# Feed-forward opening of a two-layer hybrid network: the casts of the first four weight units leave the pinned order of ACT

## The chip, the cores and the metric

The kernel runs on one core of a Trainium2 chip. The metric is the device time of one execution in microseconds (us); of several executions the median counts. The core has five engines with an instruction queue each: PE (TensorE, the matrix products; a separate row PEld shows its weight loads), DVE (VectorE), ACT (ScalarE), POOL (GpSimd) and SP (SyncE, which here only issues DMA transfers). Each engine executes its own queue in order, and engines wait for one another by semaphores.

## The reference, cut to what matters

Two layers work on 512 latent tokens and 256 context tokens of width 1024. Layer 0 mixes the tokens with an mLSTM and gated linear attention, layer 1 with an RWKV-7 recurrence. After each mixer stands a residual with two norms, and then a gated feed-forward part with a 3x3 depthwise convolution on the gate; the change touches that part's opening.

```python
def conv_ffn(h, w_up, conv_w, conv_b, w_down, grid):
    gate, up = jnp.split(h @ w_up, 2, axis=-1)
    gate = dwconv_grid(gate, conv_w, conv_b, grid)
    return (jax.nn.gelu(gate, approximate=True) * up) @ w_down

# reference(), per layer
xl = xl + mod_l[2] * rmsnorm(yl, norm_g[layer, 1])
hl = modulate(rmsnorm(xl, norm_g[layer, 2]), mod_l[3], mod_l[4])
xl = xl + mod_l[5] * rmsnorm(conv_ffn(hl, ffn_w_up[layer], ffn_conv_w[layer], ffn_conv_b[layer],
                                      ffn_w_down[layer], lat_grid), norm_g[layer, 3])
```

In layer 0 the context tokens go through the same steps; in layer 1, the last, only the latent tokens do. The width of gate and up is 2816 each.

## The kernel before, in words

**Layout.** Activations lie with the width on the 128 partitions: 8 tiles of 128 rows, the tokens along the free axis. The tokens are cut into three segments of 256 columns: CTX (context), H0 and H1 (the halves of the latent tokens). Layer 0 works on CTX, H0, H1 in this order, layer 1 on H0, H1.

**Products in three parts.** Every fp32 value is split into a high part (a cast to the matrix engine's rounded type) and a low part (value minus high part). A product is the sum of three matmuls: high by high, high weights by low activations, low weights by high activations. Activations are `mh`/`ml` in layer 0 and `zh`/`zl` in layer 1.

**A weight unit** (`unit`) is 1024 x 128 weights: SP issues the load of `wraw` (L390), ACT casts it to `whi` in two halves of 128x512 (L396), and DVE or POOL subtracts to `wlo` in two halves (L397). There are 15 buffers for such units.

**Two kinds of order.** The program is written out once, and a scheduler places the instructions of each engine by its own estimates, within the data dependences. `Ordered` is a wrapper around the engines: an ACT call made through it is handed to `keep_in_program_order`, and such ACT instructions keep the order in which they are written, among themselves; in the profile their line is that of the wrapper, L220. All other instructions are placed freely.

**The end of a mixer** (`passes`). The mixer's output projection (matmuls into `po`) goes segment by segment, and within a segment over eight output tiles m. At m = 0 of a segment the residual of the segment before is posted, at m = 7 its second norm; the last segment's residual and norm come after all products. A residual or norm begins with `rstd`: ones-matmuls add squares over the partitions (L555), DVE adds a constant (L558), POOL takes the power (L559), PE spreads the result (L561); for a norm ACT copies it (L565). The residual is then L620 and L621 (DVE, every third L621 on POOL), a store of the new stream to `xd` (L623, on SP), squares on ACT (L626) and their pair sums (L630, POOL and DVE). The norm makes the high and low parts: L590 on DVE, L594, L595, L599 on ACT, L597 on POOL, L601 on DVE. The squares for the first norm are summed on the way (L574, L577 on ACT, L578 on POOL).

**The opening burst of the feed-forward part** (`ffn`, L1094, with `projn`). Two blocks of 128 gate columns and the two matching up blocks are computed at once, so that one pass over a segment's activations serves four weight units (`UP_FIRST` = 2): units 0 and 2 subtract on DVE, 1 and 3 on POOL (`PROJN_LO`). For each segment there are 4 units x 8 tiles x 3 = 96 matmuls of 256 columns (L434, L435, L436), into PSUM tiles `pjC` (context) and `pjL` (latent). That is 288 matmuls in layer 0 and 192 in layer 1. The gate is then copied into a padded tile (`pc` or `pl`, in `act`), filtered, and put through the gelu. After the burst come the steps: blocks of up-projection (`up`) and of down-projection (`down`), with each step's weights fetched one step ahead (`fetch`).

**What is pinned before.** The wrapper is made at the top of `ffn`. So the eight casts of the opening's four units are pinned ACT instructions, as are all ACT instructions of the feed-forward part after them; those of the mixer's end before them are not.

Of the kernel before, what the change touches and what calls it, by code (L numbers as in the profile page):

```python
# [305 lines left out]
class Net:  # L306
# [787 lines left out]
    def ffn(self, layer, xh, xl, segs, y, ss, xd, post):  # L1094


        plain, I = self.nc, self.I
        nc = self.nc = Ordered(plain, self.tc)
        fw = lambda f, i: self.v("fcw", (layer * 9 + i) * NF + f, 1)
        both = len(segs) == 3  # L1100
        wide = SEGS if both else (LAT,)
# [4 lines left out]
        def act(f, acc, key, pg, pu):  # L1106
            o, w = (LAT if key == "L" else CTX)[:2]
            pl, pc = pads[f % 2]
            a = acc[:, o:o + w]
            if key == "L":  # L1110
                nc.scalar.copy(pl[:, 1:9, 1:65], pg.rearrange("p (r c) -> p r c", c=64))
                b = a.rearrange("p (r c) -> p r c", c=64)
                taps = [(i, pl[:, i // 3:i // 3 + 8, i % 3:i % 3 + 64]) for i in range(9)]
            else:
                nc.scalar.copy(pc[:, 1:257], pg[:, :w])
                b = a
                taps = [(3 + i, pc[:, i:i + 256]) for i in range(3)]
            for n, (i, src) in enumerate(taps):
                if n == 0:
                    nc.scalar.activation(b, src, AF.Identity, scale=fw(f, i), bias=self.v("fcb", layer * NF + f, 1))  # L1120
                    yield
                else:
                    nc.vector.scalar_tensor_tensor(b, src, fw(f, i), b, op0=ALU.mult, op1=ALU.add)  # L1123
            nc.scalar.activation(a, a, AF.Gelu_apprx_tanh)
            yield
            nc.vector.tensor_tensor(a, a, pu[:, :w], op=ALU.mult)

        def whole(f, acc, keys, pgs, pus):

            acts = [act(f, acc, key, pgs[key], pus[key]) for key in keys]  # L1130
            for a in acts:
                next(a)
            yield
            for a in acts:
                next(a)
            for a in acts:
                drain(a)
            h, l = self.sl("gh", dt=F32R), self.sl("gl", dt=F32R)
            gate[f] = h, l
            h, l, a = h[:, o0:T], l[:, o0:T], acc[:, o0:T]  # L1140
            nc.scalar.copy(h, a)
            yield
            (nc.gpsimd if f % 2 else nc.vector).tensor_tensor(l, a, h.bitcast(F32), op=ALU.subtract)
            done.add(f)
        live, done = [], set()

        def advance(new=None):
            k = list(live)
            if new is not None:
                next(new)  # L1150
                live.append(new)
            for g in k:
                if next(g, drain) is drain:
                    live.remove(g)
        def fetch(f0, nf, m):

            if nf:
                return self.unit(I["down"][layer, m, :, f0 * P:(f0 + nf) * P], n=nf * P)
            return [self.unit(I["up"][layer, f0, i], PROJN_LO[i]) for i in range(2)]
# [22 lines left out]
        n = UP_FIRST  # L1182
        accs = [self.sl("fa") for _ in range(n)]
        for key, psts in self.projn([I["up"][layer, i // 2, i % 2] for i in range(2 * n)], xh, xl, segs, UP_TAGS[layer]):
            if key == "C":
                acts = [act(f, accs[f], key, psts[2 * f], psts[2 * f + 1]) for f in range(n)]
                for _ in range(3):
                    for a in acts:
                        next(a, None)
                continue  # L1190
            ws = fetch(*steps[0])
            for f in range(n):
                advance(whole(f, accs[f], "L", {"L": psts[2 * f]}, {"L": psts[2 * f + 1]}))
# [952 lines left out]
```

## Time and profile before

| | |
|---|---|
| executions (three) | 2747.04, 2759.9, 2769.5 us; median 2759.9 |
| the profiled execution | 2768.18 us, of which 2766.2 us are the span |
| mean granted clock of PE | 0.939 of full speed |
| DVE busy | 1605.3 us (58%) |
| ACT busy | 1057.3 us (38%) |
| POOL busy | 970.0 us (35%) |
| read from memory, written | 213.61 MB, 37.89 MB; 91 GB/s over the span |

Below, a timeline row gives the start, the duration, the engine, the line, the operation with its output and inputs, the number of instructions drawn together, and in square brackets the engine's idle time before it with what ended that. "PE <-ACT whi L220" reads: PE was idle until ACT's cast at L220 was done. SPq rows are the issue of DMA transfers by SP. A row of windows gives a stretch's start and end, its length, the busy time of PE, PEld, DVE, ACT and POOL with the number of instructions, the granted clock of PE, the share of the DMA engines and the GB/s.

### The profile page before, as it was taken

What the parts mean: (1) busy time and instruction counts of PE and PEld (TensorE: products, weight loads), DVE (VectorE), ACT (ScalarE), POOL (GpSimd) and SP (SyncE); (2) the same over time, 40 slices, a digit from 0 to 9 for tenths busy, and PEclk for the clock granted to TensorE, in tenths of its full rate; (3) what the DMA queues carried; (4) which work ended last, traced back from release to release, by engine and by line L of the source; (5) the groups of instructions that cost most, each with busy time, mean ns of one, the idle gap of its engine ahead of it and who ended that gap; (6) DMA issues with size and microseconds to landing.
All of it is one profiled execution on the core that took longest, in us unless ns stands there. A gap on an engine that the chain in (4) does not pass through costs nothing. (4 is left out here: it accounts for less than half of the span.)

```text
span 2766.2 us, 47123 instructions
## 1 busy us (share of the span) xinstructions
PE 2529.3 (91%) x18916; PEld 2040.7 (74%) x18916; DVE 1605.3 (58%) x2915; ACT 1057.3 (38%) x2205; POOL 970.0 (35%) x1031
## 2 busy tenths in 40 slices
PE   5889999878899999997989879999999998799998
PEld 2677777767888888886756647576768777678886
DVE  4567757734554464747465374665565554676774
ACT  4543443444333232334343233433443443443332
POOL 2443355444222322246212251322222212344425
PEclk8999999998899999997999989999999998899999
DMA  6221234341212212132234453333322222333323
GB/s 226 73 83 60 70 106 146 99 159 52 78 54 59 87 37 78 54 126 73 90 109 151 153 135 80 89 86 98 86 45 65 47 69 85 107 92 94 90 84 107
DMA packets 195667, 254.57 MB, mean 92 GB/s; under 512 B 112120, under 2 KB 127864, under 8 KB 195448
## 3 DMA queue, kind: packets, MB, share of 16 engines
q1 hardware_dynamic: 195448, 251.56, 30.2%
q8 instruction: 149, 2.44, 0.4%
q14 instruction: 70, 0.57, 0.1%
HBM read 213.61 MB, written 37.89 MB: 91 GB/s over the span
## 5 line engine op out<-in xcount | busy, mean ns | idle before, releaser
L397 POOL TENSOR_TENSOR wlo<-wraw,whi 128x512 fp32r<-128x512 f32 (+1 forms) x393 | 543.2, 1404 | 890.7 <-ACT whi L220 454.8
L1123 DVE SCALAR_TENSOR_TENSOR fa<-pl,vec,fa 128x512 f32<-128x512 f32 x352 | 331.3, 948 | 181.4 <-ACT fa L220 175.0
L233 POOL TENSOR_SCALAR_AFFINE_SELECT T<-T 64x256 f32<-64x256 f32 x192 | 98.3, 514 | 270.9 <-ACT T L233 227.4
L220 ACT CAST whi<-wraw 128x512 fp32r<-128x512 f32 (+1 forms) x288 | 149.3, 581 | 68.0 <-DMA wraw<-in_up 26.2
L396 ACT CAST whi<-wraw 128x512 fp32r<-128x512 f32 x241 | 139.0, 619 | 74.0 <-DMA wraw<-in_wmod 22.2
L397 DVE TENSOR_TENSOR wlo<-wraw,whi 128x512 fp32r<-128x512 f32 x136 | 115.5, 887 | 77.8 <-ACT whi L220 34.0
L220 ACT COPY pl<-pjL 128x512 f32<-128x512 f32 x44 | 25.8, 586 | 339.4 <-PE pjL L412 304.0
L408 PE MATMUL pjL<-zh,whi 128*128 128x512 f32 x320 | 126.2, 394 | 2.2 <-ACT whi L220 2.2
L409 PE MATMUL pjL<-ml,whi 128*128 128x512 f32 x320 | 126.6, 396 | 0.0
L409 PE MATMUL pjL<-zl,whi 128*128 128x512 f32 x320 | 126.3, 395 | 0.0
L412 PE MATMUL pjL<-zh,wlo 128*128 128x512 f32 x320 | 126.1, 394 | 0.1
L408 PE MATMUL pjL<-mh,whi 128*128 128x512 f32 x320 | 126.1, 394 | 0.0
L412 PE MATMUL pjL<-mh,wlo 128*128 128x512 f32 x320 | 126.0, 394 | 0.0
L233 DVE TENSOR_SCALAR SU<-cst,el 64x64 f32<-64x64 f32 x176 | 51.1, 291 | 116.2 <-PE cst L233 113.1
L412 PE MATMUL pdL<-gh,wlo 128*128 128x512 f32 x288 | 113.8, 395 | 1.0 <-POOL wlo L397 1.0
L408 PE MATMUL pdL<-gh,whi 128*128 128x512 f32 x288 | 113.3, 394 | 0.2 <-ACT whi L220 0.2
L409 PE MATMUL pdL<-gl,whi 128*128 128x512 f32 x288 | 113.2, 393 | 0.0
L1175 DVE TENSOR_TENSOR y<-y,pdL 128x512 f32<-128x512 f32 x48 | 33.0, 687 | 108.3 <-PE pdL L412 108.2
L233 PE MATMUL pmy<-T,q0t 64*64 64x192 f32 x768 | 94.1, 349 | 0.8 <-DVE SU L233 0.8
L233 ACT ACTIVATE SU<-cst,el 64x64 f32<-64x64 f32 x176 | 53.6, 307 | 104.1 <-PE cst L233 103.6
L233 PE MATMUL ps<-bk,av 64*64 64x192 f32 x768 | 89.5, 355 | 3.5 <-DVE bk L233 1.9
L408 PE MATMUL pjC<-mh,whi 128*128 128x256 f32 x320 | 89.8, 281 | 0.0
(502 smaller groups left out, 7328.1 us busy)
## 6 DMA issues: line engine op xcount, KB each, us to landing
wraw<-in_up SPq DMA_DIRECT2D x88, 512.0 KB, 3.6
wraw<-in_wmod SPq DMA_DIRECT2D x64, 512.0 KB, 4.0
wfill<-in_wmod SPq DMA_DIRECT2D x32, 512.0 KB, 5.1
wraw<-in_rkv SPq DMA_DIRECT2D x24, 512.0 KB, 3.8
wraw<-in_win_fm SPq DMA_DIRECT2D x21, 512.0 KB, 4.4
wraw<-in_down SPq DMA_DIRECT2D x32, 320.0 KB, 2.9
xd<-y SPq DMA_DIRECT2D x64, 128.0 KB, 1.8
wraw<-in_down SPq DMA_DIRECT2D x32, 256.0 KB, 2.6
```

The costliest lines, as they stand in the source:

```text
L220: return lambda *a, **k: self.tc.keep_in_program_order(f(*a, **k))
L233: return f(*a, **k)
L396: nc.scalar.copy(hi[:, c], raw[:, c])
L397: (nc.gpsimd if lo == "pool" else nc.vector).tensor_tensor(w[:, c], raw[:, c], hi[:, c].bitcast(F32), op=ALU.subtract)
L408: nc.tensor.matmul(pst[tag][:m, :w], w1, xh[kc][:, o:o + w], start=st, stop=False)
L409: nc.tensor.matmul(pst[tag][:m, :w], w1, xl[kc][:, o:o + w], start=False, stop=False)
L412: nc.tensor.matmul(pst[tag][:m, :w], w0, xh[kc][:, o:o + w], start=False, stop=sp)
L1123: nc.vector.scalar_tensor_tensor(b, src, fw(f, i), b, op0=ALU.mult, op1=ALU.add)
L1175: nc.vector.tensor_tensor(yj, yj, pst[tag][:, :w], op=ALU.add)
```

## The change

The wrapper is no longer made at the top of `ffn` but inside the loop over the segments of the opening burst, after the first piece of that burst has been written out. `projn` calls `unit` before it yields its first piece, and by then `self.nc` is still the plain one; so the casts of the opening's four units, eight per layer and 16 in all, are not pinned any more (their line becomes L396). In layer 0 the pinned order now begins with the first copy into a pad tile, in layer 1 with the casts of step 0, which are fetched ahead of the first copy.

```diff
     def ffn(self, layer, xh, xl, segs, y, ss, xd, post):
...
-        plain, I = self.nc, self.I
-        nc = self.nc = Ordered(plain, self.tc)
+        I = self.I
+        plain = nc = self.nc
...
         for key, psts in self.projn([I["up"][layer, i // 2, i % 2] for i in range(2 * n)], xh, xl, segs, UP_TAGS[layer]):
+
+            nc = self.nc = Ordered(plain, self.tc)
             if key == "C":
```

No instruction is added or removed. What moves are the casts, and with them the loads, subtractions and matmuls that depend on them, at the opening of both feed-forward parts.

On ACT, in layer 0, around the last norm before the burst; `whi<-wraw` are the casts, `nt`, `mh` the norm of H1, `pc` the first pad copy. Before:

```order
L594 ACTIVATE nt<-nt,modT 128x256
L595 CAST mh<-nt 128x256
L220 CAST whi<-wraw 128x512 x8
L220 COPY pc<-pjC 128x256
L220 ACTIVATE fa<-pc,vec 128x256
```

After, among the work of the output projection's last segment (`y<-po` is its copy out of PSUM, `sq` and `xc` are squares); these are the casts of units 1, 2 and 3, those of unit 0 stand some rows earlier:

```order
L626 ACTIVATE xc<-y 128x256 x2
L396 CAST whi<-wraw 128x512 x2
L626 ACTIVATE xc<-y 128x256 x2
L458 COPY y<-po 128x256
L626 ACTIVATE xc<-y 128x256
L577 ACTIVATE sq<-y 128x256
L458 COPY y<-po 128x256
L577 ACTIVATE sq<-y 128x256
L396 CAST whi<-wraw 128x512 x2
L458 COPY y<-po 128x256
L577 ACTIVATE sq<-y 128x256
L396 CAST whi<-wraw 128x512 x2
```

The eight casts stood in one block behind the last norm; now they stand two by two among the copies and squares of an earlier stretch.

On SP, in layer 0: `xd_94<-y` are the 24 stores of the new stream, `in_up` the loads of the feed-forward weights, of which the first four are the opening's. Before:

```order
L610 DMA xc<-in_xT 128x768 x8
L390 DMA wraw<-in_wout 128x1024 x5
L1086 DMA wraw<-in_wout 128x1024
L390 DMA wraw<-in_up 128x1024
L623 DMA xd_94<-y 128x256 x24
L390 DMA wraw<-in_up 128x1024 x11
```

After:

```order
L390 DMA wraw<-in_up 128x1024
L623 DMA xd_94<-y 128x256 x9
L390 DMA wraw<-in_up 128x1024
L623 DMA xd_94<-y 128x256 x6
L390 DMA wraw<-in_up 128x1024
L623 DMA xd_94<-y 128x256
L390 DMA wraw<-in_up 128x1024 x2
L623 DMA xd_94<-y 128x256 x8
L390 DMA wraw<-in_up 128x1024 x7
```

Three of the opening's loads stood behind all 24 stores; now they stand behind 9, 15 and 16 of them.

On POOL, in layer 0, over the same stretch: `wlo` are the subtractions of units 1 and 3. Before:

```order
L630 TENSOR_TENSOR xc<-xc 128x256
L621 TENSOR_TENSOR y<-y,xc 128x256
L578 TENSOR_TENSOR ss<-ss,sq 128x256 x4
L559 TENSOR_TENSOR rsc<-rsc,powc 128x2 x2
L597 TENSOR_TENSOR ml<-nt,mh 128x256 x4
```

After:

```order
L630 TENSOR_TENSOR xc<-xc 128x256
L397 TENSOR_TENSOR wlo<-wraw,whi 128x512 x2
L621 TENSOR_TENSOR y<-y,xc 128x256
L578 TENSOR_TENSOR ss<-ss,sq 128x256 x3
L397 TENSOR_TENSOR wlo<-wraw,whi 128x512 x2
L578 TENSOR_TENSOR ss<-ss,sq 128x256
L559 TENSOR_TENSOR rsc<-rsc,powc 128x2 x2
```

Unit 1's two halves are now ahead of the last addition of H0's residual, and unit 3's two ahead of the last sum of squares of H1. Units 0 and 2 move on DVE into the same stretch.

On PE, in layer 0, from the end of the output projection; `rsb` are the sums and spreads of `rstd`. Before:

```order
L555 MATMUL rsb<-onek,xc 128x1 x8
L555 MATMUL rsb<-onek,ss 128x1 x2
L561 MATMUL rsb<-ident,rsc 128x128 x2
L555 MATMUL rsb<-onek,ss 128x1 x2
L561 MATMUL rsb<-ident,rsc 128x128 x2
L555 MATMUL rsb<-onek,xc 128x1 x8
L561 MATMUL rsb<-ident,rsc 128x128 x2
L434 MATMUL pjC<-mh,whi 128x256
L435 MATMUL pjC<-ml,whi 128x256
```

After:

```order
L555 MATMUL rsb<-onek,xc 128x1 x8
L555 MATMUL rsb<-onek,ss 128x1 x2
L434 MATMUL pjC<-mh,whi 128x256
L435 MATMUL pjC<-ml,whi 128x256
L436 MATMUL pjC<-mh,wlo 128x256
L434 MATMUL pjC<-mh,whi 128x256
L561 MATMUL rsb<-ident,rsc 128x128 x2
L555 MATMUL rsb<-onek,ss 128x1 x2
L435 MATMUL pjC<-ml,whi 128x256
```

The burst began behind all sums and spreads; now its context products of units 0 and 1 stand between them. Further on in the order after, 15 matmuls of H0 follow, and then the four sums of H1's second norm, with 11, 17 and 6 context matmuls of units 2 and 3 between them, 4 more ahead of their spread, and 10 behind it; the remaining 177 latent matmuls come last.

On PE, in layer 1, at the second norm of H1, its names with their numbers (`pjL_21657` to `pjL_21660` are the four units' tiles, `zh_20581` is the first tile of activations). Before:

```order
L555 MATMUL rsb_21555<-onek_80,xc_21207 128x1 x2
L555 MATMUL rsb_21555<-onek_80,xc_21209 128x1 x2
L555 MATMUL rsb_21555<-onek_80,xc_21211 128x1 x2
L555 MATMUL rsb_21555<-onek_80,xc_21213 128x1 x2
L561 MATMUL rsb_21555<-ident_74,rsc_21564 128x128 x2
L434 MATMUL pjL_21657<-zh_20581,whi_21627 128x256
```

After:

```order
L434 MATMUL pjL_21659<-zh_21137,whi_21643 128x256
L435 MATMUL pjL_21659<-zl_21138,whi_21643 128x256
L436 MATMUL pjL_21659<-zh_21137,wlo_21644 128x256
L555 MATMUL rsb_21555<-onek_80,xc_21207 128x1 x2
L434 MATMUL pjL_21658<-zh_20581,whi_21635 128x256
L435 MATMUL pjL_21658<-zl_20582,whi_21635 128x256
```

The sums stood ahead of the whole burst; now the 48 matmuls of H0 with units 0 and 2 are ahead of them, the 48 with units 1 and 3 between and behind them (7, 18, 6 between the four sums, 4 ahead of the spread, 13 behind it), and the 96 of H1 come last. On POOL and ACT the subtractions and casts of layer 1 move up likewise, to ahead of and among the residual and norm of H0, and on SP four more loads of `in_up` stand ahead of the first stores.

## The prediction

> **What bounds the kernel now.** I began with the page's busy times and then cut the span into windows, since the average says little about a stretch.
>
> ```profile
> PE 2529.3 (91%) x18916; PEld 2040.7 (74%) x18916; DVE 1605.3 (58%) x2915; ACT 1057.3 (38%) x2205; POOL 970.0 (35%) x1031
> ...
> 660.00:671.00 11.00, 11.00 (x96) 11.00 (x94) 2.90 (x5) 4.50 (x12) 6.01 (x8) 1.00 0.18 61
> 676.00:685.00 9.00, 1.22 (x4) 0.93 (x4) 9.00 (x21) 6.36 (x16) 5.22 (x7) 0.50 0.05 18
> 685.00:690.00 5.00, 3.38 (x15) 3.30 (x16) 3.75 (x6) 1.44 (x4) 2.39 (x4) 0.50 0.70 193
> 700.00:707.00 7.00, 6.56 (x30) 6.27 (x31) 6.34 (x4) 3.73 (x8) 6.89 (x7) 0.52 0.23 75
> 705.00:1225.00 520.00, 519.63 (x3056) 458.41 (x3055) 278.18 (x362) 162.57 (x307) 148.10 (x109) 1.00 0.23 71
> 2366.00:2372.00 6.00, 0.00 (x0) 0.00 (x0) 5.19 (x11) 5.26 (x13) 3.82 (x6) 0.50 0.38 156
> 2376.00:2397.00 21.00, 21.00 (x180) 21.00 (x179) 4.51 (x3) 3.06 (x6) 6.90 (x5) 1.00 0.11 37
> 2410.00:2700.00 290.00, 288.76 (x1241) 232.81 (x1242) 211.79 (x238) 112.27 (x206) 118.91 (x89) 1.00 0.31 92
> ```
>
> PE bounds it: 91% of the span, and practically all of 705 to 1225 and of 2410 to 2700, the two feed-forward parts. Just before each of them PE is nearly idle at half clock: 1.22 of 9.00 us, 3.38 of 5.00, 0 of 6. Since PE is full behind these gaps, whatever the opening burst gains reaches the end of the kernel one to one; the gaps are what to look at.
>
> The timelines of PE, ACT, POOL and SP there:
>
> ```profile
> 671.24 1.84 PE L555 MATMUL rsb<-onek,xc 128*128 128x1 f32 x16
> 674.67 0.51 PE L555 MATMUL rsb<-onek,ss 128*128 128x1 f32 x4
> 676.48 1.22 PE L561 MATMUL rsb<-ident,rsc 128*128 128x128 f32 x4 [1.31 <-POOL rsc L559]
> 685.18 1.87 PE L555 MATMUL rsb<-onek,xc 128*128 128x1 f32 x8 [7.47 <-POOL xc L630]
> 688.48 1.87 PE L555 MATMUL rsb<-onek,xc 128*128 128x1 f32 x8 [1.44 <-DVE xc L630]
> 691.46 1.22 PE L561 MATMUL rsb<-ident,rsc 128*128 128x128 f32 x4 [1.11 <-POOL rsc L559]
> 700.14 0.58 PE L434 MATMUL pjC<-mh,whi 128*128 128x256 f32 x1 [7.46 <-ACT whi L220]
> ...
> 699.47 2.70 ACT L220 CAST whi<-wraw 128x512 fp32r<-128x512 f32 x5
> 736.76 0.59 ACT L220 COPY pl<-pjL 128x512 f32<-128x512 f32 x1 [18.28 <-PE pjL L436]
> ...
> 2357.39 1.87 PE L555 MATMUL rsb<-onek,xc 128*128 128x1 f32 x8 [9.40 <-POOL xc L630]
> 2363.68 1.22 PE L561 MATMUL rsb<-ident,rsc 128*128 128x128 f32 x4 [1.11 <-POOL rsc L559]
> 2372.34 0.58 PE L434 MATMUL pjL<-zh,whi 128*128 128x256 f32 x1 [7.44 <-ACT whi L220]
> ...
> 2396.03 0.59 ACT L220 COPY pl<-pjL 128x512 f32<-128x512 f32 x1 [17.14 <-PE pjL L436]
> ...
> 658.81 0.92 POOL L597 TENSOR_TENSOR ml<-nt,mh 128x256 fp32r<-128x256 f32 x1
> 662.15 0.92 POOL L621 TENSOR_TENSOR y<-y,xc 128x256 f32<-128x256 f32 x1
> 680.91 1.97 POOL L597 TENSOR_TENSOR ml<-nt,mh 128x256 fp32r<-128x256 f32 x2 [1.60 <-ACT mh L595]
> ...
> 624.66 63.83 SPq L623 DMA_DIRECT2D xd<-y  x24
> 688.59 19.37 SPq L390 DMA_DIRECT2D wraw<-in_up  x6
> ...
> wraw<-in_up SPq DMA_DIRECT2D x88, 512.0 KB, 3.6
> ```
>
> In both layers the burst's first matmul (700.14, 2372.34) waits for ACT's pinned cast, which starts at 699.47, right behind the last norm. The last low part of the context was finished at 659.73 (658.81 + 0.92), H0's at 682.88: PE had data but no weights. And the loads of units 1 to 3 are issued only at 688.59, behind the 24 stores. The end of the burst is the first `pl` copy: 736.76 and 2396.03.
>
> **The casts themselves** (16) cost nothing new: 2.70 us for five, so about 0.54 us each, as before. What hides them is ACT's free time: in 660 to 671 it is busy for 4.50 of 11.00 us. If that cover failed, eight casts would cost 4.3 us per layer; the copies of `po` would be late by as much.
>
> **The loads on SP.** Units 1 to 3 now stand behind 9, 15 and 16 stores. The sixteenth waits for the last addition of H0's residual, about 663 before, and behind unit 1's subtractions now about 666. With 3.6 us from issue to landing, unit 3 lands near 670 and is cast by 671.5. The eight stores now behind the loads feed nothing near. I book nothing.
>
> **The subtractions on POOL and DVE** do lie in a chain that counts. Rows for their price, and for POOL's last sum of H1's squares:
>
> ```profile
> 669.64 0.74 POOL L578 TENSOR_TENSOR ss<-ss,sq 128x256 f32<-128x256 f32 x1 [2.15 <-ACT sq L577]
> 701.20 6.40 POOL L397 TENSOR_TENSOR wlo<-wraw,whi 128x512 fp32r<-128x512 f32 x4
> 700.12 6.34 DVE L397 TENSOR_TENSOR wlo<-wraw,whi 128x512 fp32r<-128x512 f32 x4 [1.14 <-ACT whi L220]
> ```
>
> One half costs 1.6 us on either engine while both work at it. Unit 3's two (3.2 us) now precede that last sum: started at 671.5 they end at 674.7, the sum at 675.4 instead of 670.4. PE took it at 674.67 at the latest, so the slack of 4.3 us eats most of the 5.0. I take 1.5 us of delay for H1's residual; the ends are 0, if the unit lands as the slack needs, and 5, if the slack is gone. In layer 1 unit 3's halves stand about the power of a norm and step 0's inside the norm of H0: three or four halves, 5 to 6 us of POOL, part of it in POOL's pauses; I take 2 us, ends 0 and 6.
>
> The Trainium skill, "SBUF — State Buffer", section "SBUF: two separate sides", says that a vector operation with two SBUF inputs and a GpSimd operation exclude each other for a whole instruction; by it each subtraction would also block the other engine's norm work. The rows agree in that both engines' halves took 1.6 us together.
>
> **The burst in layer 0.** Rates first: at full clock 21.00 us for 180 matmuls, 0.117 us each; at half clock twice that, 0.233, as a bound. How the clock behaves while PE is fed thinly is seen where layer 0 passes into layer 1, an opening that is interleaved with sums already:
>
> ```profile
> 1285.00:1290.00 5.00, 2.84 (x10) 1.95 (x10) 5.00 (x9) 1.42 (x4) 4.94 (x6) 0.50 0.13 44
> 1290.00:1295.00 5.00, 5.00 (x28) 5.00 (x29) 4.49 (x11) 2.48 (x6) 3.63 (x4) 0.61 0.19 63
> 1289.81 1.01 PE L555 MATMUL rsb<-onek,xc 128*128 128x1 f32 x4 [1.52 <-POOL xc L630]
> 1293.81 0.31 PE L435 MATMUL pjC<-vl,whi 128*128 128x256 f32 x1
> ```
>
> Busy for 57%, PE stays at half clock; unbroken from 1289.81, it comes to full clock at 1293.8, 4.0 us later (the shorter matmuls start there). I therefore charge each wait of PE with a stretch of 4 us at half clock, which loses half of it, 2 us.
>
> After the change PE does 48 context matmuls and 15 of H0 between 673 and 685, under the norm of H0. Then H1's sums: the first, at 685.18 before, comes at 686.7. From there in PE's order: 38 context matmuls among and behind the sums up to the spread, then 10, then 177 latent ones, 225 in all, times 0.117 is 26.3 us; sums and spread 2 x 1.87/2 + 1.22/2 at full clock are 2.5 us, waits for the chain 2 us, one stretch of 4 us at half clock 2 us. 686.7 + 26.3 + 2.5 + 2 + 2 = 719.5. H1's activations are not late for that: its spread, at 691.46 before, comes near 694, its norm 8.7 us later (691.46 to 700.14), at 703; by then PE, with 10 and 81 matmuls of H0 to do first (10.6 us), is at about 705. So the copy comes at 719 instead of 736.76: 17.5 us won.
>
> The Trainium skill, "TensorE: Matmul & The Clock Gate", section "Part 1: The HAM clock gate (the "warmup" mystery)", has the array throttled only after an idle window of about 3.4 us. By it the clock would stay full in this opening, and the term would be some 2 us larger, an estimate from that page. The rows above differ: at 1285 to 1290 waits no longer than that kept it at 0.50.
>
> **The burst in layer 1.** H0's 96 matmuls fill 2348 to 2368, under the two chains. H1's spread, at 2363.68 before, comes 2 us later, at 2365.7; its activations begin 2 to 3 us behind it. So its 96 matmuls run from 2369: 11.2 us at 0.117, 2 us for the half clock, and 1 us of waiting for the last tiles: 2383 instead of 2396.03, 13 us won.
>
> **The sum** is 17.5 + 13 = 30.5. The profiled execution took 2768.2 us, so 2737.7; it lies 0.3% above the median of the three, 2759.9, against which I give the forecast: 2729.
>
> **Rivals.** *The chain is later than I think.* If POOL's halves, the port and PE's own order (a sum now stands behind up to 17 matmuls, 4.0 us at half clock) cost H1's second norm 8 us in layer 0 and 6 in layer 1, and PE, having done all else, waits for it, the gains shrink to about 10 and 7: 2743. For it speaks that POOL does the power, the sums and the subtractions in one queue; against it that PE has 91 matmuls of H0 left in layer 0 to cover it.
>
> *The clock does not come up.* At 0.233 the 225 matmuls take 52.4 us and end near 743, no gain; layer 1's 96 take 22.4 and end near 2392, 4 us won: 2756. Against it stands the row at 1293.8.
>
> *Slower.* ACT's queue is in order: a freely placed cast whose load is not there yet holds the `po` copies behind it, and with them the projection itself. Unit 3's cast stands two copies ahead of the projection's end. It turns into a loss once the load comes over 30 us late (17.5 + 13 won otherwise), eight times the 3.6 us that a landing takes; at 35 us late it would be 2764.
>
> That the change does nothing is excluded by the orders: PE's first burst matmul now stands ahead of the spreads.
>
> **How the numbers follow.** My forecast gets 0.61 (its own range 2720 to 2738: gains of 22 to 40, from the ends of the two delays, 0 and 5, 0 and 6, and one wait of PE more or less per layer), the late chain 0.27, the clock 0.08, slower 0.04. A measurement of this kernel tells about 1% from no change, 27.6 us. Of my forecast about 0.14 lies within that (gains of 22 to 27.6), so faster by over 1% is 0.47, within 1% 0.49, slower by over 1% 0.04. The range 2715 to 2750 leaves out the clock and the slower case and a little beyond each end.
>
> **What would show it.** Right: the first `pjC` matmul at 673 to 675; the first `pl` copy near 719 and 2383; H1's spreads near 694 and 2366; PE at full clock by about 691 and by 2373; behind the copies everything as before, only earlier. Wrong: PE waiting over 3 us for `mh` or `zh` of H1 (late chain); 0.50 past 700 (clock); casts that wait for a load with `po` copies behind them (slower).

## The result, and the profile after

| | before | after |
|---|---|---|
| median of four executions each | 2760.11 us | 2727.32 us |
| lowest and highest | 2747.04, 2769.5 | 2724.26, 2732.1 |
| span of the profiled execution | 2766.2 us | 2722.5 us |
| mean granted clock of PE | 0.939 | 0.949 |

The ratio is 0.988 with a 95% interval of [0.9854, 0.9906]: the kernel became faster by 1.2%, 33 us of median.

The page's busy times after the change:

```profile
PE 2519.5 (93%) x18916; PEld 2035.5 (75%) x18916; DVE 1593.0 (59%) x2915; ACT 1055.6 (39%) x2205; POOL 969.2 (36%) x1031
```

Windows around layer 0's opening, with the columns as before:

```profile
671.00:676.00 5.00, 4.85 (x22) 4.56 (x22) 5.00 (x12) 3.77 (x9) 2.55 (x3) 0.50 0.02 5
676.00:685.00 9.00, 9.00 (x76) 9.00 (x75) 8.42 (x17) 4.14 (x12) 5.61 (x7) 0.97 0.33 113
685.00:690.00 5.00, 4.47 (x39) 4.26 (x37) 0.79 (x3) 0.48 (x2) 0.71 (x1) 1.00 0.70 217
690.00:700.00 10.00, 10.00 (x87) 10.00 (x86) 7.96 (x17) 8.94 (x20) 5.19 (x8) 1.00 0.01 2
```

PE does the same number of instructions in 9.8 us less busy time, at a mean granted clock of 0.949 instead of 0.939. The hole ahead of the feed-forward part is filled: from 676 to 685 PE is busy for 9.00 us where it had 1.22, at a clock of 0.97 instead of 0.50, and from there on the clock is full, to the end of the rows shown.

The timelines of PE, ACT, POOL and SP in the changed kernel, both openings:

```profile
665.54 1.84 PE L555 MATMUL rsb<-onek,xc 128*128 128x1 f32 x16
668.43 0.61 PE L555 MATMUL rsb<-onek,ss 128*128 128x1 f32 x4 [1.04 <-POOL ss L578]
668.89 0.37 PE L434 MATMUL pjC<-mh,whi 128*128 128x256 f32 x1
681.17 0.50 PE L555 MATMUL rsb<-onek,xc 128*128 128x1 f32 x4
688.15 0.71 PE L561 MATMUL rsb<-ident,rsc 128*128 128x128 f32 x4 [0.53 <-POOL rsc L559]
...
664.49 1.14 ACT L396 CAST whi<-wraw 128x512 fp32r<-128x512 f32 x2 [0.95 <-DMA wraw<-in_up]
710.00 0.59 ACT L220 COPY pl<-pjL 128x512 f32<-128x512 f32 x1 [8.21 <-PE pjL L436]
...
665.18 2.51 POOL L397 TENSOR_TENSOR wlo<-wraw,whi 128x512 fp32r<-128x512 f32 x2 [0.66 <-ACT whi L396]
667.64 0.73 POOL L578 TENSOR_TENSOR ss<-ss,sq 128x256 f32<-128x256 f32 x1
...
2328.07 0.61 PE L555 MATMUL rsb<-onek,xc 128*128 128x1 f32 x4 [1.52 <-POOL xc L630]
2334.77 0.84 PE L555 MATMUL rsb<-onek,xc 128*128 128x1 f32 x4
2337.88 0.71 PE L561 MATMUL rsb<-ident,rsc 128*128 128x128 f32 x4 [0.53 <-POOL rsc L559]
...
2351.29 0.59 ACT L220 COPY pl<-pjL 128x512 f32<-128x512 f32 x1 [5.79 <-PE pjL L436]
...
620.48 27.88 SPq L623 DMA_DIRECT2D xd<-y  x9
648.63 0.33 SPq L390 DMA_DIRECT2D wraw<-in_up  x1
657.50 0.40 SPq L390 DMA_DIRECT2D wraw<-in_up  x1
660.75 0.88 SPq L390 DMA_DIRECT2D wraw<-in_up  x2
```

The first burst matmul stands right behind the sums of the output projection, no longer behind ACT's cast, and the three late loads are issued at 648.63, 657.50 and 660.75 instead of 688.59.

The spans of the two profiles differ by 43.7 us, the medians by 32.8. To see which part belongs to the change I cut every profile at three marks: the first store of layer 0's residual (`xd<-y`), the first `pl` copy of each layer, and the last loads of layer 1's output projection (`in_rwo`). The kernels of the lower rows are those of the next section.

| kernel | until the first store | layer 0's opening: store to copy | copy to `in_rwo` | layer 1's opening: `in_rwo` to copy | copy to end |
|---|---|---|---|---|---|
| before | 624.7 | 112.1 | 1557.1 | 102.2 | 370.2 |
| before, again | 622.7 | 110.3 | 1553.3 | 102.3 | 370.1 |
| after | 620.5 | 89.5 | 1550.7 | 90.6 | 371.2 |
| after, again | 620.3 | 90.5 | 1551.5 | 88.9 | 369.7 |
| layer 0 only | 621.5 | 89.7 | 1550.3 | 103.6 | 371.6 |
| layer 1 only | 614.5 | 112.0 | 1553.5 | 88.6 | 371.0 |
| loads behind the stores | 619.2 | 99.1 | 1551.1 | 95.4 | 370.0 |
| sums first, layer 1 | 619.9 | 89.9 | 1550.0 | 91.7 | 369.8 |
| step 0 late, layer 1 | 621.2 | 89.7 | 1550.2 | 85.0 | 370.1 |
| step 0 late, timed | 626.2 | 91.2 | 1552.0 | 85.2 | 370.2 |
| step casts free | 625.1 | 94.3 | 1549.1 | 89.3 | 366.7 |
| all on POOL | 623.3 | 92.6 | 1564.2 | 89.0 | 370.8 |
| step casts free and late, layer 1 | 617.9 | 89.7 | 1557.9 | 85.2 | 368.5 |

The two openings account for 22.6 + 11.6 = 34.2 us of the first pair of profiles and for 19.8 + 13.4 = 33.2 us of the second, which is the gain of the medians; the other 9.5 us of the first pair lie where the orders are alike, and these stretches move by themselves: the first store by 12 us over the thirteen profiles, the long stretch between the openings by 14 (1550.0 to 1564.2) over the twelve that have the same order there. (With all step casts free it is another order.)

### The profile page after: what moved, and what is told of

It reads as the page before. It is cut to its first block, busy times and chain, and to the rows that moved or that the text cites. A ratio compares the mean times of both kernels' runs of the same rounds, so it can differ in the third digit from the quotient of the medians.

```text
span 2722.5 us, 47114 instructions
## 1 busy us (share of the span) xinstructions
PE 2519.5 (93%) x18916; PEld 2035.5 (75%) x18916; DVE 1593.0 (59%) x2915; ACT 1055.6 (39%) x2205; POOL 969.2 (36%) x1031
## 3 DMA queue, kind: packets, MB, share of 16 engines
q1 hardware_dynamic: 195448, 251.56, 30.7%
## 4 chain that ended last, share of the span: by engine, by line
PE 37%; DVE 6%; DMA 2%; issue 2%; ACT 2%; POOL 1%; SPq 0%; POOLq 0%; DVEq 0%; ACTq 0%
PE pmg L233 4%; PE ps L233 3%; PE pjL L412 3%; PE pjL L408 3%; PE pjL L409 3%; PE pmt L233 3%; PE pmy L233 2%; PE cst L233 2%; PE mfill L233 2%; PE pk L233 2%; DVE leaf L233 2%; PE wo L233 1%; PE pdL L412 1%; PE pdL L409 1%; PE pdL L408 1%
## 5 line engine op out<-in xcount | busy, mean ns | idle before, releaser
L396 ACT CAST whi<-wraw 128x512 fp32r<-128x512 f32 x257 | 148.1, 619 | 74.6 <-DMA wraw<-in_wmod 21.5
L220 ACT CAST whi<-wraw 128x512 fp32r<-128x512 f32 (+1 forms) x272 | 140.9, 579 | 67.1 <-DMA wraw<-in_up 31.2
L397 DVE TENSOR_TENSOR wlo<-wraw,whi 128x512 fp32r<-128x512 f32 x136 | 109.7, 842 | 77.2 <-ACT whi L220 32.2
L233 PE MATMUL pmy<-T,q0t 64*64 64x192 f32 x768 | 91.7, 343 | 0.8 <-DVE SU L233 0.8
```

What stands on the lines that cost most here:

```text
L220: return lambda *a, **k: self.tc.keep_in_program_order(f(*a, **k))
L233: return f(*a, **k)
L396: nc.scalar.copy(hi[:, c], raw[:, c])
L397: (nc.gpsimd if lo == "pool" else nc.vector).tensor_tensor(w[:, c], raw[:, c], hi[:, c].bitcast(F32), op=ALU.subtract)
```

## The experiments

One detail of the pin is needed here: an ACT call through the wrapper is tied behind the ACT instruction written just ahead of it, whether that one is pinned or not. The first pinned cast was therefore tied to the last cast of the norm of H1. No run takes this apart, but the orders agree with it: before, the eight casts stand directly behind that cast; in the changed kernel, the first pad copy (695.25) is ahead of it (695.50).

**The changed kernel again**, as the mark for three others on the same chip:

> The changed kernel once more, as the mark for the others on the same chip. Every theory: the ratio to the kernel before again 0.985 to 0.991, about 33 us.

Ratio 0.9872 [0.9851, 0.9893], medians 2722.43 and 2757.93 us: as in the first measurement.

**Each layer alone.** In layer 0 only (for layer 1 only, with `layer == 1`):

```diff
-        plain = nc = self.nc
+        plain = self.nc
+        nc = self.nc = plain if layer == 0 else Ordered(plain, self.tc)
```

> Casts unpinned in layer 0 alone; layer 1's opening stays as before. If the gain is made at the two openings and each is worth what the traces show there (22.5 and 11.6 us), this kernel gains 22 us (ratio 0.992), its layer 0 opening ends (first pl copy) some 22 us earlier against the first store than before, and nothing moves between the openings. The rival: part of the gain comes from the stretch between the openings (the two profiles differ by another 6 us there); then this kernel gains 27 us or more, and its stretch from the first pl copy of layer 0 to the first load of layer 1's opening is some 6 us shorter than before.

> Casts unpinned in layer 1 alone. By the openings alone: 11 to 12 us gained (ratio 0.996). By the rival (part of the gain lies elsewhere): under 8 us, with both kernels together short of the whole change's 33 by 6 us or more.

Layer 0 alone: ratio 0.9936 [0.9919, 0.9953], 18.4 us of median, less than the 22 us expected, which lie at the edge of the interval. Layer 1 alone: 0.9957 [0.9941, 0.9973], 12.3 us. Together 30.7, against 35.5 for both on that chip: within the intervals the parts add up. Layer 0's opening is 20.6 to 22.4 us shorter than in the two profiles of before, and layer 1's is 13.6 us shorter where it was changed, and not where it was not. The stretch between the openings was 6.8 us shorter in the kernel with layer 0 alone, which by itself would speak for the rival; but the gain of 18.4 us does not, and the next run takes the mark away.

**The kernel before, profiled again:**

> The kernel before, profiled once more, to see how far its stretches move by themselves. If the 6 us between the openings are the run and not the change: the stretch from layer 0's first pl copy to the loads of layer 1's projection (1557.1 us before, 1550.7 after) comes out 3 us or more off 1557; if they are the change's: 1556 to 1558. The openings (first store to first pl copy 112.1 us; projection loads to first pl copy 102.2) within 1 us of before by either.

1553.3 us: 3.8 us off by itself, and the two openings 1.8 and 0.04 us off. (The bound of 1 us for the openings was too tight for layer 0's.) Later runs of kernels with layer 0 changed gave 1564.2 and 1557.9 in that stretch. What moves there is seen in windows from mark to mark, of before, of the changed kernel, and of the longest, with all four units on POOL:

```profile
736.76:2293.82 1557.06, 1470.92 (x13119) 1177.38 (x13117) 876.29 (x1775) 564.78 (x1214) 453.86 (x581) 0.95 0.30 85
710.00:2260.71 1550.71, 1465.18 (x13119) 1174.54 (x13117) 874.05 (x1775) 564.54 (x1214) 454.78 (x581) 0.95 0.30 86
715.85:2280.00 1564.15, 1479.05 (x13119) 1183.21 (x13117) 876.10 (x1775) 565.85 (x1214) 458.82 (x581) 0.95 0.30 85
```

PE does the same 13119 matmuls in each and is idle for 85 to 86 us in each; what differs is how long the matmuls take. The trace's clock records give a mean granted clock of 0.951, 0.955 and 0.945 there: the longer stretch is the one in which PE ran at half clock for longer. So most of the difference belongs to the run. That a part of some 3 us goes with the change isn't excluded: the three profiles with layer 0 as before took 1553.3 to 1557.1 us, eight of the ten others 1549.1 to 1552.0.

**Casts free, loads behind the stores.** The loads of units 1 to 3 are queued on SP behind the last store:

```diff
-                nc.sync.dma_start(xdst[:, j, o:o + w], yj)
+                self.last_xd = nc.sync.dma_start(xdst[:, j, o:o + w], yj)
...
+            with self.tc.issue_after(self.last_xd.ins) if held and i else nullcontext():
+                us.append(self.unit(s, PROJN_LO[i % len(PROJN_LO)]))
...
```

> Casts unpinned in both layers as in the change, but the loads of units 1 to 3 are issued behind the last store of the residual, as before. Theory: the gain hangs on the weights being there during the two norms, so the loads must move too; only unit 0 is early here, PE does its matmuls in the gap and the other three units' behind the last norm: 7 to 9 us gained in layer 0, 3 to 5 in layer 1, some 12 in all (ratio 0.9955). Rival: PE's wait was named as one for ACT's cast, so freeing the cast suffices and the loads come along in time: the whole 33 us (0.988). Other rival: without the loads nothing is gained, 0 to 3 us.

Ratio 0.9941 [0.9923, 0.9958], 16 us of median; the openings got 13.0 and 6.8 us shorter against the first profile of before. Both rivals fall: with the loads held back about half of the gain is left, so the early loads carry the other half. (The reverse, early loads with the casts still pinned, was not run.) My sizes were too low. SP, ACT and PE of this kernel in layer 0:

```profile
681.62 37.94 SPq L390 DMA_DIRECT2D wraw<-in_up  x9
...
693.69 2.18 ACT L396 CAST whi<-wraw 128x512 fp32r<-128x512 f32 x4
...
695.05 0.38 PE L439 MATMUL pjC<-mh,wlo 128*128 128x256 f32 x1 [0.38 <-POOL wlo L397]
```

The loads start at 681.62, the four last casts at 693.69, and PE still takes its context products at 695 and later. In before, the chain from load to matmul was hidden behind the pinned cast: the trace names only the releaser that came last, and in its shadow the loads were late too.

**All four units on POOL.** The subtractions of units 0 and 2 move from DVE to POOL, PE's order is unchanged:

```diff
-        us = [self.unit(s, PROJN_LO[i % len(PROJN_LO)]) for i, s in enumerate(src)]
+        us = [self.unit(s, "pool" if up else PROJN_LO[i % len(PROJN_LO)]) for i, s in enumerate(src)]
...
```

> The changed kernel with the subtractions of all four opening units on POOL, in both layers, so that POOL's load in the residual and norm chain doubles. PE's order is unchanged. Theory: in layer 0, 187 matmuls stand behind H1's spread in PE's order, 21.9 us at 0.117, so that the first pl copy follows the spread by 21.9 us and a later spread is a later copy one to one; four more halves of 1.3 to 1.6 us on POOL, of which some lie in its pauses, make the opening 2 to 6 us longer (first store to copy 92 to 96 us, against 89.5 to 90.5). Rival: H0's matmuls cover the delay; the opening stays within 1 us of 90 and the spread comes closer to the copy.

POOL, PE and ACT of this kernel:

```profile
669.95 2.49 POOL L397 TENSOR_TENSOR wlo<-wraw,whi 128x512 fp32r<-128x512 f32 x2
672.39 0.73 POOL L578 TENSOR_TENSOR ss<-ss,sq 128x256 f32<-128x256 f32 x1
...
694.00 0.71 PE L561 MATMUL rsb<-ident,rsc 128*128 128x128 f32 x4 [0.54 <-POOL rsc L559]
...
715.85 0.59 ACT L220 COPY pl<-pjL 128x512 f32<-128x512 f32 x1 [8.21 <-PE pjL L436]
```

The spread comes 70.8 us behind the first store (67.7 in the changed kernel), the copy 92.6 us (89.5): 3.1 us each. From the spread to the copy it is 21.85 us in both, and in the six other profiles with layer 0 as in the change, whose spreads come at 67.9 to 69.4 us. So PE's queue passes a late spread on to the copy one to one, and the work behind it covers nothing. How late POOL made it is less sure: 1.4 to 3.1 us against these seven profiles, by one profile of its own.

**The chain in layer 1.** There the spread of H1 came 77.2 us behind the `in_rwo` loads, against 69.9 before, 7.3 us late (75.5 in its second profile, 75.2 with layer 1 alone changed). Two runs divide this. First, PE's order: the H0 matmuls of units 1 and 3 are held behind the four sums.

```diff
...
+                        with self.tc.issue_after(self.last_sum.ins) if held and i % 2 and o == H0[0] else nullcontext():
                             nc.tensor.matmul(ps[:, cs], hi[:, ks], xh[kc][:, xs], start=kc == 0, stop=False)
...
```

> The changed kernel, but in layer 1 PE does the H0 matmuls of units 1 and 3 only behind the four sums of H1's second norm. Theory: 3.5 us of the spread's delay in layer 1 come from sums that stand behind up to 18 matmuls at half clock; here the time from the first sum to the spread falls from 9.8 to about 6.3 us, as before, but 48 matmuls move behind the spread (5.6 us), so that the first pl copy comes at the same time, within 2 us, or later. Rival: the delay comes from POOL and DVE; then first sum to spread stays at 9 us or more.

The sums and the spread of this kernel:

```profile
2327.11 0.61 PE L556 MATMUL rsb<-onek,xc 128*128 128x1 f32 x4 [1.52 <-POOL xc L631]
...
2329.87 1.87 PE L556 MATMUL rsb<-onek,xc 128*128 128x1 f32 x8 [0.88 <-DVE xc L631]
2332.86 1.22 PE L562 MATMUL rsb<-ident,rsc 128*128 128x128 f32 x4
```

5.75 us from first sum to spread, less than the 6.29 of before, against 9.81 in the changed kernel (8.27 in the two other profiles with this opening); and the copy is not earlier (91.7 us against 88.6 to 90.6), since 48 matmuls now follow the spread. As the theory had it: the delay by PE's order is real, and PE spends it on work that has to be done anyway.

Second, step 0: its casts, and with them its subtractions, are held behind the last norm's ACT work.

```diff
...
-            ws = fetch(*steps[0])
+            with self.tc.issue_after(self.last_norm.ins) if layer == 1 else nullcontext():
+                ws = fetch(*steps[0])
```

> The changed kernel, but in layer 1 step 0's casts stand behind the last norm on ACT, and so their subtractions too. Theory: step 0's casts and subtractions inside H0's norm cost the chain 2.7 us (first sum 3.8 us late against before, of which 1.1 come from unit 3's subtractions at the power); here the first sum is 1 to 1.5 us late only, and the first pl copy comes 1.5 to 3 us earlier than in the changed kernel (projection loads to copy 90.6 us there, 88 to 89 here). Rival: unit 3's subtractions and PE's order make the delay; then the copy moves by less than 1 us.

```profile
2325.62 0.61 PE L555 MATMUL rsb<-onek,xc 128*128 128x1 f32 x4 [0.26 <-POOL xc L630]
2332.67 0.71 PE L561 MATMUL rsb<-ident,rsc 128*128 128x128 f32 x4 [0.53 <-POOL rsc L559]
...
2360.40 0.50 PE L408 MATMUL pjL<-zh,whi 128*128 128x512 f32 x1 [2.23 <-ACT whi L220]
...
2325.62:2332.67 7.05, 6.52 (x54) 6.32 (x54) 3.75 (x7) 1.45 (x4) 2.95 (x4) 1.00 0.70 221
```

The changed kernel from first sum to spread:

```profile
2328.07:2337.88 9.81, 9.28 (x52) 9.07 (x52) 1.63 (x5) 1.33 (x4) 2.90 (x4) 0.65 0.22 74
```

The first sum comes 64.5 us behind the loads, 1.0 late instead of 3.8, as expected. The gain at the copy is larger: 85.0 us, 3.6 to 5.6 less than in three profiles with the change (88.6 to 90.6), and it goes with the clock: PE waits only 0.26 us for that sum instead of 1.52, and the matmuls between the sums then run at a clock of 1.00 instead of 0.65. Timed:

> The kernel with step 0's casts behind the last norm in layer 1, now timed. Theory: 4 to 5 us faster than the changed kernel, ratio 0.9855; rival: one profile was lucky, ratio 0.987 to 0.988 as for the changed kernel.

Ratio 0.985 [0.9829, 0.9871], opening 85.2 us. The opening's gain is there again; by the time alone it can't be told from the changed kernel, whose two intervals overlap with this one.

**The next pinned casts.** The last row above shows a wait that the changed kernel has as well, 14 us behind the copy; its row there:

```profile
2365.60 0.50 PE L408 MATMUL pjL<-zh,whi 128*128 128x512 f32 x1 [2.42 <-ACT whi L220]
```

In the next kernel the casts of all up-projection steps are unpinned too:

```diff
-            return [self.unit(I["up"][layer, f0, i], PROJN_LO[i]) for i in range(2)]
+            self.nc = plain
+            r = [self.unit(I["up"][layer, f0, i], PROJN_LO[i]) for i in range(2)]
+            self.nc = nc
+            return r
```

> The changed kernel, with the casts of all up-projection steps unpinned too. In the changed kernel PE still waits 2.4 us for a pinned cast (whi, line 220) some 14 us behind layer 1's first pl copy, and runs at half clock after it. Theory (a pinned cast holds back weights that could be there): that wait goes, 3 to 5 us gained in layer 1 against the changed kernel. Rival: the freed casts bring step 0's subtractions into layer 0's norms as well, as they did in layer 1, and H1's spread comes later there; then layer 0's opening gets longer by 2 to 5 us and the whole is no faster.

Ratio 0.9887 [0.9863, 0.9911]: no faster than the changed kernel. Both theories hold, one in each layer. The wait is gone, and behind layer 1's copy 366.7 us remain instead of 369.7 to 371.2; layer 0's opening takes 94.3 instead of 89.5 to 90.5. POOL in layer 0 shows why:

```profile
682.28 0.87 POOL L597 TENSOR_TENSOR ml<-nt,mh 128x256 fp32r<-128x256 f32 x1 [1.60 <-ACT mh L595]
683.11 1.14 POOL L559 TENSOR_TENSOR rsc<-rsc,powc 128x2 f32<-128x2 f32 x1
684.22 2.52 POOL L397 TENSOR_TENSOR wlo<-wraw,whi 128x512 fp32r<-128x512 f32 x2
```

The power of H1's residual, at 671.13 in the changed kernel, stands behind three L597 of H0's norm, and two subtractions of step 0 follow it ahead of the fourth. The first sum of H1's second norm comes 64.8 us behind the first store, against 60.7 to 62.3 in the seven profiles with layer 0 as in the change.

**Both together, in layer 1 only:** layer 0 as in the change; in layer 1 all step casts unpinned, but queued behind the last norm.

```diff
...
+            if layer == 0:
+                return [self.unit(I["up"][layer, f0, i], PROJN_LO[i]) for i in range(2)]
+            self.nc = plain
+            with self.tc.issue_after(self.last_norm.ins):
+                r = [self.unit(I["up"][layer, f0, i], PROJN_LO[i]) for i in range(2)]
+            self.nc = nc
+            return r
```

> Layer 0 as in the change; in layer 1 the casts of all up-projection steps are unpinned, and they and step 0's stand behind the last norm's ACT work. Theory: the two gains of the runs before add up: 4 to 5 us in the opening (step 0's subtractions out of the chain, projection loads to first pl copy 85 us) and 4 us behind it (no wait for a pinned cast, copy to end 366.5 us), some 8 us against the changed kernel, ratio 0.984. Rival: both take from the same wait, and the second is smaller once step 0 comes later; 4 to 5 us in all, ratio 0.9855.

Ratio 0.9825 [0.9798, 0.9851], medians 2715.47 and 2766.04 us: the lowest ratio of all. The opening is 85.2 us as in the timed run above, the wait behind the copy is gone; but the rest takes 368.5 us, 1.3 to 2.7 less than with the change and not 4 less. The ratio suits the first theory, the stretches lie between the two. Against the changed kernel by itself it wasn't timed on one chip; against the kernel with step 0 alone held late, on the same chip, its median is 8 us lower, with overlapping intervals.

## Why the prediction was right

The time came out at 2727.3 where 2729 was forecast, and each opening is what paid: 22.6 and 11.6 us in the first pair of profiles, 19.8 and 13.4 in the second, against 17.5 and 13 in the sum. That the total lies within 2 us of the forecast is in part luck: layer 0 was forecast too low by 2 to 5 us, and layer 1 came out by two errors that cancel. The steps, one by one; times of the changed profile are moved onto before's clock by the first store (4.2 us) or the `in_rwo` loads (33.1 us).

- *PE had data but no weights*: right. The first burst matmul came at 673.1 (forecast 673 to 675).
- *Loads and casts book nothing*: right. One cast of unit 3 waited 0.95 us for its load (664.49), with two `po` copies behind it, and the projection still ended no later than before. The third of the late loads was issued at 664.9, where I had put it near 666. Without the early loads half of the gain is lost, so this move, to which the prediction gave a paragraph with a price of nothing, carries as much as the cast.
- *Chain in layer 0, 1.5 us late at the first sum, spread near 694*: 0.2 us late and spread at 692.3 in the first pair; by all profiles about 1 us, with the first sum 59.0 to 60.5 us behind the first store where layer 0 is as before and 60.7 to 62.3 where it is as in the change. Unit 3's two halves took 2.5 us and not 3.2, and POOL's last sum ended at 672.6, 2.2 us later than before and not 5, well within the slack of 4.3.
- *The burst in layer 0*: the gain was forecast too small by about 5 us, against the first pair. I took 32.8 us from first sum to copy; it was 28.8: the 26.3 of matmuls, 1.9 of sums and spread and 0.5 of waiting. Of the 2 us for waits 1.5 were not spent, and none of the 2 us for a stretch at half clock: that stretch fell ahead of the first sum. The clock had dropped near 670 (0.50 from 671 to 676 of its own profile) and was full again from 676.6 on, in a run of context matmuls that began at 669. The remaining 1.3 us are the chain's.
- *Layer 1: H1's spread 2 us late*: wrong in size, 7.3 us (5.3 to 5.6 in the two other profiles with this opening). 3.8 are there at the first sum, mostly step 0's casts and subtractions inside H0's norm (without them 1.0); the other 3.5 (2.0 in the two others) come between first sum and spread, from matmuls at half clock ahead of the sums (held back, 5.75 us instead of 9.8; at full clock, with step 0 late, 7.05). What I had booked for these was 2 us, within ends of 0 and 6.
- *Layer 1's copy at 2383*: 2384.4, by two errors that cancel. The spread was 5.3 us later than forecast, but from there to the copy it took 13.4 us, not 17.3: PE had 13 H0 matmuls to fill the norm's start, and ran at full clock. So the right time of this copy is luck.
- *The late chain as a rival, with 91 matmuls of H0 against it*: in layer 1 the chain was as late as this rival had it (7.3 us against 6), but the gain did not shrink to 7 us; in layer 0 it was 0.9 us late at the spread, not 8. Its sign, PE waiting over 3 us for H1's `mh` or `zh`, did not show in either layer. The argument against it was wrong all the same: those 91 matmuls stand behind the spread in PE's queue and wait with it, and a later spread was a later copy one to one.
- *Clock* and *slower* fall: the clock was full past 685 and from 2338, and no load came later than the 0.95 us above.

Ahead of these times the clock did drop, once in each opening. Windows of the changed kernel in layer 1:

```profile
2324.00:2330.00 6.00, 3.44 (x22) 3.03 (x21) 4.69 (x10) 1.42 (x5) 5.47 (x7) 0.89 0.26 87
2330.00:2335.00 5.00, 5.00 (x26) 5.00 (x25) 0.85 (x2) 0.94 (x4) 0.26 (x1) 0.50 0.32 105
2335.00:2338.00 3.00, 2.47 (x18) 2.27 (x19) 0.16 (x1) 0.00 (x0) 0.71 (x1) 0.92 0.00 0
2338.00:2340.00 2.00, 2.00 (x17) 1.93 (x17) 0.90 (x3) 0.75 (x2) 0.00 (x0) 1.00 0.00 0
```

With PE busy for 3.44 of 6 us the clock falls, and the next 5 us of solid work run at 0.50. In layer 0 it fell near 670, after a stretch from 666 to 670 with 2.96 of 4.00 us busy; through 685 to 690, with 4.47 of 5.00 us busy, it stood at 1.00. So the charge of 2 us per wait was the wrong form: these three stretches suggest that what counts is how much of a stretch of several us is idle. The Trainium skill, "TensorE: Matmul & The Clock Gate", section "Part 1: The HAM clock gate (the "warmup" mystery)", ties the drop to an idle window of about 3.4 us. Taken as a single wait of that length, neither opening agrees: the longest single wait ahead of the drop was 1.52 us in layer 1 and 1.04 us in layer 0. In layer 0 one doubt is left: the 16 sums ahead of that wait have one column each, and whether such matmuls count as work for the clock no run here shows. The prediction's own row against that rule, 1285 to 1290, shows a clock that stayed low and not one that fell.

## What to carry to other kernels

A wait names its last releaser only: before a pin or a dependence is taken away, look at what else arrives late behind it (here the loads behind 24 stores, worth half of the gain), since a freed instruction helps as far as its inputs come early too. Work that is let into an idle stretch lands in the queues of the engines that end the stretch: four more POOL subtractions ahead of the power that PE waits for made it some 1.4 to 3.1 us later, and the copy with it one to one, so free what the idle engine can use now, and hold the next step's work behind the chain. When profiles differ by more than the medians, cut them at marks and compare the stretches whose order is the same: they show how much of a difference is the run.

## What the runs showed of the hardware that was not expected

In layer 1 the clock fell from full to 0.50 without any single wait over 1.52 us, after a stretch of 6 us in which PE was 57% busy, and was full again 6.8 us later though PE worked without a pause from the fall on; in layer 0 it fell after a longest wait of 1.04 us, also for 6.8 us. With 89% busy it stayed up. In the clock records of the kernel before, of the changed one and of the one with all units on POOL, the granted clock is either 1.00 or 0.50, and each stretch at one of them lasts a multiple of 3.41 us. Between the openings the same matmuls in the same order took 1550.0 to 1564.2 us over twelve profiles, 0.9%, nearly half of the whole change; in the three shown, PE's idle time is alike within 1.1 us, and the time at half clock makes the difference.
